# A decoder trunk on one core: layer 0's rows of split activations on another pitch and offset

## The chip, the cores and the metric

One core of a Trainium2 chip. The metric is the device time in microseconds of one execution of the whole program; of the kernel before there are three such runs. One more execution was recorded by the hardware profiler, and all lines of the profile come from that one.

## The reference

Two decoder layers over a sequence of 16 meta tokens and 256 tokens (272 positions), width 2048, 16 heads of 128, an MLP of 8192. All arithmetic is float32. Cut to its core:

```python
for layer in range(2):
    a = rms_norm(h, norm_attn[layer])
    if layer == 0:
        q, k, v, f_logit = split(a @ fox_w_in)          # 2048 x (3*2048 + 16)
        o = forgetting_attention(q, k, v, cumsum(log_sigmoid(f_logit + b_f)))
        h = h + o @ fox_w_o
    else:
        k, v = split(rms_norm(h, kv_norm) @ w_kv)        # 2048 x 4096
        o = stick_breaking_attention(a @ sb_w_q, k, v)
        h = h + o @ sb_w_o
    h = h + square(relu(rms_norm(h, norm_mlp[layer]) @ w_up[layer])) @ w_down[layer]
return rms_norm(h, final_norm)[:, 16:]
```

Layer 0, and the keys and values of layer 1, are computed for all 272 positions; the queries, the output projection and the MLP of layer 1 for the last 256 alone.

## The kernel before

Everything is held feature-major: a tile has 128 features on the partitions and the positions side by side along the partition. A stream of width 2048 is 16 chunks of 128 features.

**Split numbers.** The large products run as three matmuls in fp32r, a form of float32 of which the high part of a number is kept. A weight block is loaded by DMA into `raw` (SP's queue, L202), ScalarE rounds it to `whi` (L213) and VectorE subtracts to get the rest, `wlo` (L214). Activations are split in the same way into `hi` and `lo` (`split_chunk` at L130 and L131, `put_split` at L356 and L357, the MLP's own lines L499 and L500). A product is then whi·hi + whi·lo + wlo·hi, added up in PSUM.

**The rows.** Class `Split` holds both parts of a stream: for each chunk c one row of `XROW` = 576 floats on every partition, with hi from float 16 on and lo directly behind it. With t0 = 0 a part has n = 272 columns, with t0 = M = 16 it has 256:

```python
rows = xs.tile([P, NC, XROW], F32R, tag="x", name=f"x_{label}")
self.hi, self.lo = rows[:, :, XHI:XHI + n], rows[:, :, XHI + n:XHI + 2 * n]
self.both = rows[:, :, XHI:XHI + 2 * n]
```

Pool `xs` has two buffers, which the streams use in turn: x_a (the input of attention), x_o (its output), x_m (the input of the MLP), x_u (four quarters of its inner activations), x_kv (the input of the shared keys and values). The buffer `ob` of the final output comes from the same pool.

**The products.** `gemm_group` (L178) computes 512 output features: 16 chunks of contraction in four blocks `kb`, four output tiles `m`, each with a PSUM tile `acc`. All its matmuls are recorded at L172, in an order that is pinned behind one another. For 272 columns the order is chunk by chunk whi·hi, whi·lo, wlo·hi (L243 to L245). For the 256-column streams (`pairs`) hi and lo lie side by side, so that one matmul of 512 columns (`both`) does whi·hi and whi·lo at once; the 256-column matmuls with wlo follow after the chunks of the run (L231 to L238). The last tile of the last group alone is computed unpaired.

**Order of the work.** The queries, keys and values of layer 0 are computed in groups of four heads, with the small matmuls of attention between them; then output projection, four quarters of the MLP (up, then down), and the same for layer 1. The order on each engine is made by a scheduler when the program is built. All weight tiles have four buffers, so loads and splits run ahead of the matmuls.

**Scratch.** The program reserves 16 KB at the start of each partition for descriptors of DMAs that are written in software; the tiles follow behind it.

Of the kernel before, what the change touches and what calls it, by code (L numbers as in the profile page):

```python
# [9 lines left out]
F32 = mybir.dt.float32  # L10
F32R = mybir.dt.float32r
# [4 lines left out]
P = 128  # L16
D = 2048
NC = D // P
M = 16
# [3 lines left out]
BIG = 1.0e30  # L23
QSCALE = 1.0 / math.sqrt(P)
N_FF = 4
XROW = 576
XHI = 16

G_A0, G_M0, G_KV, G_A1, G_M1, G_FIN = range(6)

# [2 lines left out]
def yoco_kernel(ctx: ExitStack, tc: tile.TileContext, hT_in, gains, b_f, w_f, w_qkv0, w_o0, w_up, w_dn,  # L33
                w_kv, w_q1, w_o1, outT):
    nc = tc.nc
# [6 lines left out]
    xs = ctx.enter_context(tc.tile_pool(name="xs", bufs=2))  # L42
# [74 lines left out]
    class Split:  # L117


        def __init__(self, label, t0):  # L120
            n = T - t0
            self.t0 = t0
            rows = xs.tile([P, NC, XROW], F32R, tag="x", name=f"x_{label}")
            self.hi, self.lo = rows[:, :, XHI:XHI + n], rows[:, :, XHI + n:XHI + 2 * n]
            self.both = rows[:, :, XHI:XHI + 2 * n]

    def split_chunk(sp, gi, c):

# [523 lines left out]
    a, y, t, rs = (fin[:, i, :] for i in range(4))  # L652
# [9 lines left out]
    for i in range(2):  # L662
# [2 lines left out]
            nc.tensor.matmul(pr[:, b * P:(b + 1) * P], rs[:, b:b + 1].to_broadcast([P, P]), ident,  # L665
                             start=True, stop=True)
        prs.append(pr[:, :S])
    ob = xs.tile([P, NC, XROW], F32, tag="x", name="ob")
    pr_sb = tmp.tile([P, T], F32, tag="relu", name="pr_sb")[:, :S]
    nc.scalar.copy(pr_sb, prs[1])  # L670
    for c, n in [(12, 1), (13, 1), (14, 1), (15, 1), (0, 2), (2, 2), (4, 2), (6, 2)]:
# [62 lines left out]
```

## Time and profile before

| | before |
|---|---|
| three runs, us | 2332.77, 2333.07, 2332.89 (median 2332.89) |
| profiled execution, us | 2332.09 |
| its span, first to last instruction, us | 2330.3 |
| granted TensorE clock | 0.998 |
| matmuls | 16,486 |
| busy: TensorE, VectorE, ScalarE, GpSimd | 100%, 58%, 46%, 2% |
| bytes moved by DMA, mean rate | 412.00 MB, 177 GB/s |

Of a matmul the profile gives the start and a duration. The duration runs from the start to the modelled end and overlaps the next matmul, so a stream of matmuls is read by the distance of their starts. In the timeline neighbouring instructions of one kind are merged into one row: start, length of the merged row, engine, line, operation, tiles and number.

Three stretches on the span's scale: layer 0 with its MLP until about 1208 us (its MLP from about 444 us on), the queries, keys, values and attention of layer 1 until about 1532 us, and output projection and MLP of layer 1 until 2318 us.

### The profile page before, as it was taken

Reading aid. Unit: us, or ns where it says so; the run is one execution under the profiler, and the core shown is the slowest. Engines: PE = TensorE matmul, PEld = TensorE weight load, DVE = VectorE, ACT = ScalarE, POOL = GpSimd, SP = SyncE. Lnnn points to the kernel's source line nnn. Section 1 sums busy time; section 2 is a strip of 40 time slices with the busy share of each in tenths; the row PEclk is TensorE's granted clock in tenths of the full one; section 3 lists DMA queues with packets and bytes.
Section 4 is the critical chain, followed back from the end, with each engine's and each line's share of the span. In section 5 each row is a group of like instructions: output and inputs, shape, how many; then the busy total and the mean of one; then the engine's idle time right before and its main releaser. Section 6 shows DMA issues by size and latency. Waiting matters only on the chain.

```text
span 2330.3 us, 39954 instructions
## 1 busy us (share of the span) xinstructions
PE 2319.3 (100%) x16486; PEld 2200.1 (94%) x16486; DVE 1350.6 (58%) x1923; ACT 1064.8 (46%) x1477; POOL 38.9 (2%) x58
## 2 busy tenths in 40 slices
PE   9999999999999999999999999999999999999998
PEld 9999999999999999999998999988888888888887
DVE  7665555654454455445566555566665665655665
ACT  6434344543344344334455444455543543543553
POOL 1000000000000000000000000000000000000000
PEclk9999999999999999999999999999999999999999
DMA  6544545455545555555556444446556556555553
GB/s 233 172 155 163 169 158 171 166 185 173 180 168 185 176 174 180 172 182 172 181 175 198 160 145 145 145 163 199 184 190 198 186 187 199 185 191 195 185 198 128
DMA packets 116630, 412.00 MB, mean 177 GB/s; under 512 B 13264, under 2 KB 16736, under 8 KB 116448
## 3 DMA queue, kind: packets, MB, share of 16 engines
q1 hardware_dynamic: 114560, 406.29, 52.4%
q10 hardware_dynamic: 1888, 3.16, 0.4%
q8 instruction: 129, 2.11, 0.4%
q14 instruction: 53, 0.43, 0.1%
HBM read 407.29 MB, written 2.11 MB: 176 GB/s over the span
## 4 chain that ended last, share of the span: by engine, by line
PE 99%; DVE 0%; ACT 0%; issue 0%; DVEq 0%; ACTq 0%
PE acc L172 96%; PE ps L402 0%; PE pza L581 0%; PE pv L335 0%; PE po L464 0%; PE po L620 0%; PE idle L60 0%; PE pzb L582 0%; PE po L621 0%; PE po L465 0%; PE po L622 0%; DVE ob L676 0%; PE pf L301 0%; PE pf L302 0%; PE pta L597 0%; PE pta L596 0%
## 5 line engine op out<-in xcount | busy, mean ns | idle before, releaser
L214 DVE TENSOR_TENSOR wlo<-raw,whi 128x1024 fp32r<-128x1024 f32 (+1 forms) x773 | 931.7, 1217 | 752.6 <-ACT whi L213 751.7
L213 ACT ACTIVATE whi<-raw 128x1024 fp32r<-128x1024 f32 (+1 forms) x773 | 799.2, 1050 | 960.4 <-PE acc L172 939.9
L172 PE MATMUL acc<-x_u,whi 128*128 128x272 f32 (+2 forms) x3088 | 650.8, 322 | 0.0
L172 PE MATMUL acc<-x_m,whi 128*128 128x272 f32 (+1 forms) x3072 | 649.2, 323 | 0.0
L172 PEld LDWEIGHTS acc<-x_u,whi 128*128 128x128 f32 x3088 | 497.4, 188 | 26.3
L172 PEld LDWEIGHTS acc<-x_m,whi 128*128 128x128 f32 x3072 | 495.5, 188 | 26.9
L172 PE MATMUL acc<-x_u,wlo 128*128 128x272 f32 (+1 forms) x2048 | 441.7, 280 | 0.0
L172 PE MATMUL acc<-x_m,wlo 128*128 128x272 f32 (+1 forms) x2048 | 439.4, 280 | 0.0
L172 PE MATMUL acc<-x_a,whi 128*128 128x272 f32 (+1 forms) x1792 | 363.0, 307 | 0.0
L172 PEld LDWEIGHTS acc<-x_u,wlo 128*128 128x128 f32 x2048 | 339.5, 188 | 15.9
L172 PEld LDWEIGHTS acc<-x_m,wlo 128*128 128x128 f32 x2048 | 338.5, 188 | 16.1
L172 PEld LDWEIGHTS acc<-x_a,whi 128*128 128x128 f32 x1792 | 283.5, 188 | 9.3 <-issue 0.7
L172 PE MATMUL acc<-x_a,wlo 128*128 128x272 f32 (+1 forms) x1024 | 252.9, 284 | 0.0
L172 PE MATMUL acc<-x_kv,whi 128*128 128x272 f32 x1024 | 195.8, 289 | 0.0
L172 PEld LDWEIGHTS acc<-x_a,wlo 128*128 128x128 f32 x1024 | 179.3, 188 | 4.7 <-issue 0.5
L172 PE MATMUL acc<-x_o,whi 128*128 128x272 f32 (+1 forms) x768 | 163.1, 323 | 0.0
L172 PEld LDWEIGHTS acc<-x_kv,whi 128*128 128x128 f32 x1024 | 159.9, 188 | 0.4
L172 PE MATMUL acc<-x_kv,wlo 128*128 128x272 f32 x512 | 145.9, 285 | 0.0
L252 DVE TENSOR_TENSOR hT<-acc,hT 128x256 f32<-128x256 f32 (+1 forms) x239 | 102.5, 429 | 72.0 <-PE acc L172 70.3
L172 PEld LDWEIGHTS acc<-x_o,whi 128*128 128x128 f32 x768 | 124.0, 188 | 6.7
L172 PE MATMUL acc<-x_o,wlo 128*128 128x272 f32 (+1 forms) x512 | 110.8, 282 | 0.0
L172 PEld LDWEIGHTS acc<-x_kv,wlo 128*128 128x128 f32 x512 | 96.2, 188 | 0.1
(226 smaller groups left out, 1038.5 us busy)
## 6 DMA issues: line engine op xcount, KB each, us to landing
raw<-w_up SPq DMA_DIRECT2D x256, 512.0 KB, 4.7
raw<-w_dn SPq DMA_DIRECT2D x256, 512.0 KB, 4.8
raw<-w_qkv SPq DMA_DIRECT2D x92, 512.0 KB, 4.1
raw<-w_o SPq DMA_DIRECT2D x64, 512.0 KB, 4.5
raw<-w_kv SPq DMA_DIRECT2D x64, 512.0 KB, 3.9
raw<-w_q SPq DMA_DIRECT2D x32, 512.0 KB, 4.7
fk<-f_dram ACTq DMA_DIRECT2D x4, 544.0 KB, 5.4
raw<-w_qkv SPq DMA_DIRECT2D x7, 256.0 KB, 4.7
```

The source lines that it names most:

```text
L172: ins = nc.tensor.matmul(*args, **kw).ins
L213: on_act = nc.scalar.activation(hp, src, AF.Copy)
L214: on_dve = nc.vector.tensor_tensor(out=lp, in0=src, in1=hp.bitcast(F32), op=ALU.subtract)
L252: nc.vector.tensor_tensor(out=hT[:, c, t0:], in0=a, in1=hT[:, c, t0:], op=ALU.add)
```

## The change

The rows get a pitch and two offsets of their own for each t0. For the 272-column streams a row has 640 floats (2560 bytes), hi starts at float 48 (byte 192) and lo at float 368 (byte 1472, which is 5 x 256 + 192), so that a gap of 48 floats lies between the parts. For the 256-column streams pitch and offsets stay at 576, 16 and 272 floats. Both kinds share the buffers, which become 16 x 640 + 64 floats long instead of 16 x 576, and `ob` takes the new pitch too. The scratch for software descriptors becomes 1 KB.

```diff
-XROW = 576
-XHI = 16
+ROWS = {0: (640, 48, 368), M: (576, 16, 272)}
+XROW = 640
...
-            rows = xs.tile([P, NC, XROW], F32R, tag="x", name=f"x_{label}")
-            self.hi, self.lo = rows[:, :, XHI:XHI + n], rows[:, :, XHI + n:XHI + 2 * n]
-            self.both = rows[:, :, XHI:XHI + 2 * n]
+            rows = xs.tile([P, NC * XROW + 64], F32R, tag="x", name=f"x_{label}")
+            pitch, hi, lo = ROWS[t0]
+            rows = rows[:, hi:hi + NC * pitch].rearrange("p (c t) -> p c t", c=NC)
+            self.hi, self.lo = rows[:, :, :n], rows[:, :, lo - hi:lo - hi + n]
+            self.both = rows[:, :, :2 * n]
...
-    ob = xs.tile([P, NC, XROW], F32, tag="x", name="ob")
+    ob = xs.tile([P, NC * XROW + 64], F32, tag="x", name="ob")[:, :NC * XROW].rearrange("p (c t) -> p c t", c=NC)
...
-    nc = bacc.Bacc("TRN2", target_bir_lowering=False, num_devices=1)
+    nc = bacc.Bacc("TRN2", target_bir_lowering=False, num_devices=1, dynamic_dma_scratch_size=1024)
```

## The prediction, made before the changed kernel was run

> **What bounds the kernel now.** I read the page first (busy shares, clock, the chain that ended last), then the groups kept apart by shape, the waits, and last the timeline of TensorE in one stretch of each layer.
>
> ```profile
> span 2330.3 us, 39954 instructions
> PE 2319.3 (100%) x16486; PEld 2200.1 (94%) x16486; DVE 1350.6 (58%) x1923; ACT 1064.8 (46%) x1477; POOL 38.9 (2%) x58
> ...
> PEclk9999999999999999999999999999999999999999
> ...
> q1 hardware_dynamic: 114560, 406.29, 52.4%
> q10 hardware_dynamic: 1888, 3.16, 0.4%
> ...
> PE 99%; DVE 0%; ACT 0%; issue 0%; DVEq 0%; ACTq 0%
> ```
>
> TensorE is busy for the whole span at a granted clock of 0.998, and 99% of the chain is TensorE itself: it waits for nobody. The two queues that carry nearly all bytes are hardware queues of SP and ACT. The waits say the same from the other side: the engines that prepare the weights wait for TensorE to give buffers back.
>
> ```profile
> ACT whi L213 <- PE acc L172: 939.9, 482, 4.5
> ```
>
> So time moves only if matmuls follow each other faster or slower. How fast they do is not in the mean duration of a matmul (288 ns, which overlaps its neighbours) but in the spacing of their starts. TensorE in layer 0, where one chunk is whi times hi, whi times lo, wlo times hi (the first two are merged into the "x2" rows):
>
> ```profile
> 700.06 0.28 PE L172 MATMUL acc<-x_m,wlo 128*128 128x272 f32 x1
> 700.18 0.41 PE L172 MATMUL acc<-x_m,whi 128*128 128x272 f32 x2
> 700.44 0.28 PE L172 MATMUL acc<-x_m,wlo 128*128 128x272 f32 x1
> 700.56 0.41 PE L172 MATMUL acc<-x_m,whi 128*128 128x272 f32 x2
> 700.81 0.28 PE L172 MATMUL acc<-x_m,wlo 128*128 128x272 f32 x1
> 700.93 0.41 PE L172 MATMUL acc<-x_m,whi 128*128 128x272 f32 x2
> ```
>
> First column: start in us. From 700.06 to 700.81 are six matmuls, 0.75 us, or 125 ns each; over all 1,024 triples of the x_m rows the raw starts give 373.4 ns a triple, 124.4 ns a matmul. Inside a triple the spacing is not even: a wlo matmul is followed after 0.12 us, the two whi matmuls take 0.25 to 0.26 together. In the raw starts, means: 126.7 ns from whi·hi to whi·lo, 125.8 ns from whi·lo to wlo·hi, 120.9 ns from wlo·hi to the next whi·hi. Column count, weights' size and clock are the same; what differs is where the moving rows stand.
>
> **The addresses.** In the built programs both row buffers begin at a multiple of 256 bytes, before and after. Before, the pitch is 2304 bytes (9 x 256), hi starts 64 and lo 64 + 1088, that is 128, bytes behind a multiple of 256. So the first two spacings lie between rows that stand differently (64 to 128, 128 to 64), the short one between rows that stand alike (64 to 64). After, the pitch is 2560 (10 x 256) and both parts stand at 192: all three spacings are between equals. A row of 272 columns is 1088 bytes; from 192 it ends exactly on a multiple of 256.
>
> **The change part by part.** The programs before and after hold the same instructions in the same order on all five engines; nothing is added, moved or made to wait. Left are four things.
>
> 1. *Layer 0's rows.* They feed the 272-column matmuls of x_a (layer 0's), x_o, x_m, x_u and x_kv: by the groups 1536+768, 512+256, 2048+1024, 2048+1024 and 1024+512, together 10,752, or 3,584 triples. If all three spacings become the equal-standing one, a triple takes 3 x 120.9 = 362.7 ns instead of 373.4: 10.7 ns x 3,584 = 38 us less, all of it on the path. The x_a and x_kv triples keep the same spacing between their attention stretches, so they count in full; the 32 gate matmuls (L301, L302) add 0.1 us at most. Bounds: the best spacing that any row suggests is the timeline's 0.120, which is 4.4 ns less than 124.4, x 10,752 = 48 us less; the worst is every spacing at 126.7 ns, 2.3 ns x 10,752 = 24 us more. I take 120.9, because it is measured on the same shapes.
>
> What is late next if TensorE gains 2%? Nothing: ACT and DVE are busy 46% and 58%, whi preparation idles 940 us waiting for TensorE, and the weight queue takes 52% of the DMA engines.
>
> 2. *ACT and DVE write the rows elsewhere* (L130/L131, L356/L357, L499/L500; 0.42 us each). Their cost at 192 is not in the trace. There are about 250 of them in layer 0's rows (two for each of 16 chunks in x_a, x_m, x_kv and four x_u, 24 in x_o). If each changed by a tenth, 0.04 us, that is 10 us over two engines that idle over 40% of the span: 0, unless they become the last to finish a chunk.
>
> 3. *Scratch of 1 KB instead of 16.* It serves DMAs with descriptors written in software; the page lists only hardware and instruction queues. All tiles move down by 15,360 bytes, and those behind the rows up again by 8,704: multiples of 256, so layer 1's rows, the weights and the attention tiles stand as before. 0.
>
> 4. *The output buffer* has the wider pitch: ten DMAs and ten writes in the last 9 us, rows of 1024 bytes as before. 0, at most 0.1 us either way.
>
> The profiled execution took 2332.09 us, its span 2330.3 and 1.8 around it; the median shown is 2332.89. 2332.09 - 38.3 = 2293.8; against the median 2294.6. I forecast **2294 us**.
>
> **Where this may fail: layer 1.** There all rows stand at 64, equal already:
>
> ```profile
> 1705.33 1.11 PE L172 MATMUL acc<-x_u,wlo 128*128 128x256 f32 x8
> 1706.27 2.00 PE L172 MATMUL acc<-x_u,whi 128*128 128x512 f32 x8
> 1708.10 1.07 PE L172 MATMUL acc<-x_u,wlo 128*128 128x256 f32 x8
> 1709.01 1.99 PE L172 MATMUL acc<-x_u,whi 128*128 128x512 f32 x8
> ```
>
> The same eight wlo matmuls take 0.94 us once (117.5 ns each) and 0.91 the next time (113.8). In the raw starts 46% of the 256-column matmuls run at 113.3 and 50% at 117 to 118.5, and whole runs keep to one of the two. So equal standing does not by itself give the short spacing: there is also a phase into which a run falls.
>
> **Rivals.**
> - *Half-caught phase* (a smaller gain): the good spacing 46% of the time, 0.46 x 48 = 22 us, 2311 us. For it: the two wlo runs above. Against: layer 1 alternates 512 and 256 columns, layer 0 repeats one shape.
> - *No effect.* Where a row starts is indifferent, and the short third spacing only gives back what the first two lost. For it: per triple only the sum is paid, and layer 1's slower wlo spacing, 117.8 for 256 columns, plus 16 columns at 229/512 = 0.45 ns is 125.0, nearly the 124.4 that layer 0's mixed rows pay. 2333 us. [...]
> - *The rear start is dear* (slower). A row that starts at 192 has only 64 bytes before the next multiple of 256, so the first fetch of each matmul brings 16 columns, if fetches go by such blocks. Place: the start of every layer 0 matmul; price: the dearest spacing, 126.7 ns, on all: 24 us more, 2357 us. It decides as soon as the mean spacing passes 124.4 ns. For it: every spacing that touches the row at 128 is 5 ns dearer than the one that does not. Against: the dear spacing before whi·lo and the one behind it are alike, which fits a change of standing better than a bad start.
> [...]
>
> **How the numbers follow.** Full gain 0.43 (2285 to 2300, of it 0.08 for a gain past any row), half-caught 0.18, no effect 0.14, slower 0.25. The likeliest case alone is 2285 to 2311 with its half-caught form. The range: at the bottom the 48 us bound less half a nanosecond of rounding in 0.120 (0.5 x 10.752 = 5 us), 2280; at the top the slower rival's 2357, made 2358. About one in ten lies on either side. 0.2% of the time, 4.7 us, is about what a measurement of this kernel can tell from no change: faster 0.61, same 0.14, slower 0.25.
>
> **What would show it.** In the profile after: TensorE still 100% busy, clock 0.998, instruction counts the same. In layer 0's timeline all three matmuls of a chunk evenly 0.12 apart, a chunk in 0.36 us instead of 0.373; the group of 6,000 matmuls in the chain between 445 and 1209 us shorter by some 22 us; layer 1's eight wlo matmuls still at 0.91 or 0.94. Even spacings at 0.124 would mean no effect; above 0.126 the rear start; a mixture of long and short runs the phase. A new wait of TensorE for wlo, or a changed layer 1, would make my accounting wrong altogether.

## The result, and the profile after

The changed kernel takes 2323.3 us (median of six runs, 2323.03 to 2323.93); the kernel before took 2332.83 beside it. The ratio is 0.996, 95% interval 0.9947 to 0.9973: faster, by 9.5 us where 38 were forecast. The profiled execution took 2323.63 us. Its page, the lines that answer to those shown of before:

```profile
span 2321.9 us, 39954 instructions
PE 2310.8 (100%) x16486; PEld 2190.4 (94%) x16486; DVE 1350.6 (58%) x1923; ACT 1064.0 (46%) x1477; POOL 39.9 (2%) x58
...
PEclk9999999999999999999999999999999999999999
...
q1 hardware_dynamic: 114560, 406.29, 51.4%
q10 hardware_dynamic: 1888, 3.16, 0.4%
...
PE 99%; DMA 0%; DVE 0%; ACT 0%; issue 0%; DVEq 0%; SPq 0%; ACTq 0%
```

Same instructions (39,954), same clock (0.998 of it granted in both), TensorE still the bound. From the waits, ScalarE still waits for TensorE, by some 62 us less:

```profile
ACT whi L217 <- PE acc L176: 877.4, 472, 4.1
```

The timeline of TensorE in the MLP of layer 0 (first column: start; L176 is the old L172):

```profile
700.13 0.28 PE L176 MATMUL acc<-x_m,wlo 128*128 128x272 f32 x1
700.25 0.41 PE L176 MATMUL acc<-x_m,whi 128*128 128x272 f32 x2
700.50 0.29 PE L176 MATMUL acc<-x_m,wlo 128*128 128x272 f32 x1
700.62 0.41 PE L176 MATMUL acc<-x_m,whi 128*128 128x272 f32 x2
700.87 0.28 PE L176 MATMUL acc<-x_m,wlo 128*128 128x272 f32 x1
```

From 700.13 to 700.87 are six matmuls in 0.74 us, where it was 0.75. The spacing is now even, as forecast, but not at the forecast value: the raw starts (the start times as the trace has them, to the nanosecond) give 123.3 to 123.5 ns at each of the three places of a triple, not 120.9. A triple is the three matmuls of one chunk.

The best ruler for a whole stage is a row of the chain in order of time (start, length). One unbroken run has 6,112 matmuls: 6,048 of the 6,144 of layer 0's MLP, which begins at 432.4 us before, and the first 64 of layer 1's queries. Another has 4,020 in the MLP of layer 1. Before:

```profile
444.98 763.71 PE acc L172 x6112
...
1620.80 692.00 PE acc L172 x4020
```

After:

```profile
442.52 757.05 PE acc L176 x6112
...
1610.15 693.91 PE acc L176 x4020
```

Layer 0's run is 6.7 us shorter, and layer 1's, whose rows kept their place, 1.9 us longer. Summed over the distances of all starts: layer 0 and x_kv 1351.9 to 1340.6 us (-11.3), layer 1's other streams 885.2 to 887.4 (+2.2), all other matmuls +0.8. Together this is -8.3, nearly all of the spans' difference of 8.4.

### The profile page after: what moved, and what is told of

Same layout as the page of the kernel before. It is cut to its first block, busy times and chain, and to the rows that moved or that the text cites. A ratio compares the mean times of both kernels' runs of the same rounds, so it can differ in the third digit from the quotient of the medians.

```text
span 2321.9 us, 39954 instructions
## 1 busy us (share of the span) xinstructions
PE 2310.8 (100%) x16486; PEld 2190.4 (94%) x16486; DVE 1350.6 (58%) x1923; ACT 1064.0 (46%) x1477; POOL 39.9 (2%) x58
## 4 chain that ended last, share of the span: by engine, by line
PE 99%; DMA 0%; DVE 0%; ACT 0%; issue 0%; DVEq 0%; SPq 0%; ACTq 0%
PE acc L176 95%; PE ps L406 0%; PE pza L585 0%; PE pv L339 0%; PE po L468 0%; PE po L624 0%; DMA raw<-w_qkv 0%; PE po L625 0%; PE pzb L586 0%; PE po L469 0%; DMA hT<-hT_in 0%; PE po L626 0%; DVE ob L680 0%; PE pf L306 0%; PE pf L305 0%; PE pta L600 0%
## 5 line engine op out<-in xcount | busy, mean ns | idle before, releaser
L176 PE MATMUL acc<-x_u,whi 128*128 128x272 f32 (+2 forms) x3088 | 647.5, 321 | 0.0
L176 PE MATMUL acc<-x_m,whi 128*128 128x272 f32 (+1 forms) x3072 | 646.1, 322 | 0.0
L176 PEld LDWEIGHTS acc<-x_u,whi 128*128 128x128 f32 x3088 | 499.9, 188 | 26.7
L176 PEld LDWEIGHTS acc<-x_m,whi 128*128 128x128 f32 x3072 | 497.8, 188 | 27.4
L176 PE MATMUL acc<-x_u,wlo 128*128 128x272 f32 (+1 forms) x2048 | 445.9, 282 | 0.0
L176 PE MATMUL acc<-x_m,wlo 128*128 128x272 f32 (+1 forms) x2048 | 443.7, 282 | 0.0
L176 PE MATMUL acc<-x_a,whi 128*128 128x272 f32 (+1 forms) x1792 | 360.6, 306 | 0.4 <-ACT x_a L134 0.2
L176 PEld LDWEIGHTS acc<-x_u,wlo 128*128 128x128 f32 x2048 | 340.3, 188 | 15.7
L176 PEld LDWEIGHTS acc<-x_m,wlo 128*128 128x128 f32 x2048 | 339.5, 188 | 15.9
L176 PEld LDWEIGHTS acc<-x_a,whi 128*128 128x128 f32 x1792 | 284.4, 188 | 9.9 <-issue 0.7
L176 PE MATMUL acc<-x_a,wlo 128*128 128x272 f32 (+1 forms) x1024 | 254.5, 286 | 0.0
L176 PE MATMUL acc<-x_kv,whi 128*128 128x272 f32 x1024 | 194.1, 288 | 0.0
L176 PEld LDWEIGHTS acc<-x_a,wlo 128*128 128x128 f32 x1024 | 179.6, 188 | 4.9 <-issue 0.5
L176 PE MATMUL acc<-x_o,whi 128*128 128x272 f32 (+1 forms) x768 | 162.3, 322 | 0.0
L176 PEld LDWEIGHTS acc<-x_kv,whi 128*128 128x128 f32 x1024 | 160.6, 188 | 0.4
L176 PE MATMUL acc<-x_kv,wlo 128*128 128x272 f32 x512 | 147.3, 288 | 0.0
L176 PEld LDWEIGHTS acc<-x_o,whi 128*128 128x128 f32 x768 | 124.3, 188 | 6.8
L176 PE MATMUL acc<-x_o,wlo 128*128 128x272 f32 (+1 forms) x512 | 111.6, 283 | 0.0
L176 PEld LDWEIGHTS acc<-x_kv,wlo 128*128 128x128 f32 x512 | 96.5, 188 | 0.1
```

Of the source, the lines that this page charges most:

```text
L176: ins = nc.tensor.matmul(*args, **kw).ins
```

## The experiments

All are variants of the changed kernel. The place of rows and weights is given in bytes behind a multiple of 256; in the changed kernel the weights whi and wlo stand at 0. The distance between rows and weights is the difference of their places, again modulo 256. Rows are "equal" when hi and lo have the same place, and "mixed" when they have not. "Run of layer 0" and "run of layer 1" are the two chain rows, each from the one profiled execution of its kernel. The expectations count in units of 0.417 ns, which they call cycles; no run shows a step of that length. 304, 298.7 and 296 of them are 126.7, 124.4 and 123.3 ns, and go with runs of layer 0 of 777, 764 and 757 us.

### Is it equal standing, or 192?

```diff
-ROWS = {0: (640, 48, 368), M: (576, 16, 272)}
+ROWS = {0: (640, 16, 336), M: (576, 16, 272)}    # both_at_64
+ROWS = {0: (640, 0, 320), M: (576, 16, 272)}     # both_at_0
+ROWS = {0: (640, 32, 352), M: (576, 16, 272)}    # both_at_128
+ROWS = {0: (640, 16, 288), M: (576, 16, 272)}    # wide_pitch_64_128
```

> Layer 0's hi and lo both 64 bytes behind a multiple of 256, pitch 640 floats as in the changed kernel. Theory A (equal standing is what pays, whichever the offset): spacing of layer 0's matmuls 123.3 to 123.4 ns as with 192, time 2323. Theory B (192 pays, because a row of 1088 bytes then ends on a multiple of 256 and touches one partial block): 64 has two partial blocks (192 and 128 bytes) and stays at 124.4 ns, 2333. Theory C (starts fall into a repeating pattern of their own for each offset): some other mean, 120 to 125 ns, 2290 to 2340, with layer 1 moving by a few us as well.

> Both parts at a multiple of 256. Theory A: 2323, 123.4 ns. Theory B: four whole blocks and one partial block of 64 bytes at the end, as good as 192: 2323. If the short first fetch of 192 is what helps (and not the number of blocks): worse than 192, 124.4 ns or more, 2333 or more. Theory C: some other mean, 120 to 125 ns.

> Both parts at 128. Theory A: 2323, 123.4 ns. Theory B: two partial blocks (128 at the start, 192 at the end): 124.4 ns, 2333. Theory C: some other mean, 120 to 125 ns.

> The offsets of before (hi 64, lo 128) on the new pitch of 2560 bytes, with the new scratch and buffer size: all of the change but the offsets. All theories: layer 0 at 124.4 ns. If layer 1's loss (256-column spacing 115.8 before, 116.5 after, 1.7 us) comes from its shifted buffers, it shows here too: 2334 to 2335. If it comes from the phase in which layer 0 leaves TensorE, layer 1 is as before: 2333. If the pitch itself matters, the time differs from 2333 by over 3 us.

Measured: at 64 2355.1 us (ratio 1.0095, 1.008 to 1.011), at 0 2351.7 (1.0079, 1.0064 to 1.0094), at 128 2355.5 (1.0096, 1.0079 to 1.0112), the old offsets on the new pitch 2333.2 (1.0001, 0.9991 to 1.001). The timeline of the kernel with both parts at 64:

```profile
700.19 0.29 PE L176 MATMUL acc<-x_m,wlo 128*128 128x272 f32 x1
700.32 0.42 PE L176 MATMUL acc<-x_m,whi 128*128 128x272 f32 x2
700.57 0.29 PE L176 MATMUL acc<-x_m,wlo 128*128 128x272 f32 x1
700.70 0.42 PE L176 MATMUL acc<-x_m,whi 128*128 128x272 f32 x2
700.95 0.29 PE L176 MATMUL acc<-x_m,wlo 128*128 128x272 f32 x1
```

and its run of layer 0:

```profile
450.83 777.16 PE acc L176 x6112
```

Here too the spacing is even, and six matmuls take 0.76 us: each of the three takes 126.7 ns. That is the dearest spacing of before, now at the place where before had its cheapest (64 to 64). So theory A falls, and with it the reading of the 120.9 ns: that spacing was no price of a pair of rows but a place in a pattern of which only the sum is paid. Theory B falls as well: by its own count 0 touches as few blocks as 192, and it is slow (2351.7 us against 2323.3). All three slow kernels come to the same value in layer 0's MLP (runs of layer 0 with rows at 64, 0 and 128: 777.16, 777.21, 777.16 us). Where 0 is quicker than 64 and 128, by 3.4 us and more, it is outside that run, in the x_a, x_o and x_kv rows; layer 0 and x_kv add up to 1368.9 us at 0, and to 1373.7 and 1374.4 at 64 and 128. The fourth kernel frees scratch, pitch and buffer sizes from any part in it; its run of layer 1 is 692.00 us, so layer 1's loss does not come from the moved buffers either.

### The rows' own place, or their distance to the weights?

```diff
-    pad = align.tile([P, 32], F32, name="pad")
+    pad = align.tile([P, 48], F32, name="pad")       # weights_at_64 and all_shifted_64
...
-ROWS = {0: (640, 48, 368), M: (576, 16, 272)}
+ROWS = {0: (640, 32, 352), M: (576, 0, 256)}         # weights_at_64 alone
```

> The alignment tile before the weight tiles is 64 bytes longer, so whi and wlo stand at 64 instead of 0 behind a multiple of 256; the offsets inside the rows are cut by 64 bytes, so layer 0's rows stay at 192 and layer 1's at 64. Theory D (only the moving rows' own place counts): 123.4 ns in layer 0, 2323 to 2325. Theory E (what counts is the rows' place relative to the weights that are loaded meanwhile, now 128): the spacing of the 128 rows, 126.7 ns, 2355; layer 1 (relative place 0 instead of 64) moves too.

> The alignment tile is 64 bytes longer and nothing else: weights at 64, layer 0's rows at 0, layer 1's rows at 128 behind a multiple of 256; the distances between rows and weights (192 and 64) are those of the changed kernel. Theory D (the rows' own place): layer 0 at 126.7 ns as with rows at 0, 2352. Theory E (the distance between rows and weights): 123.4 ns, 2323, and layer 1 as in the changed kernel.

Measured: with the weights alone moved 2367.8 us (1.0148, 1.0133 to 1.0163); with weights and rows moved together 2322.1 (0.9953, 0.9938 to 0.9968). The chain's runs, first of the kernel with the weights alone moved:

```profile
451.35 777.27 PE acc L176 x6112
...
1645.78 701.52 PE acc L176 x4020
```

and of the one in which all moved together:

```profile
441.79 757.03 PE acc L176 x6112
...
1609.48 692.00 PE acc L176 x4020
```

The first kernel reads its rows from exactly the places of the changed kernel (192 and 64) and loses 20 us in layer 0's run and 7.6 in layer 1's. The second has rows at 0 (layer 0) and 128 (layer 1). With the weights at 0 a place of 0 was bad in layer 0, and the last experiment will show 128 to be bad in layer 1; here nothing is lost. Theory E holds: what decides is the distance between moving rows and weights. The longer alignment tile also moves the tiles behind the rows by 64 bytes. They are not the cause: the last experiment moves wlo by 64 bytes and no other tile off its place, and layer 0 pays the same.

Moving the weights alone by 64 bytes, with the rows left in their places, cost 44 us against the changed kernel (2367.8 against 2323.3).

### How wide is the good place?

```diff
-ROWS = {0: (640, 48, 368), M: (576, 16, 272)}
+ROWS = {0: (640, 56, 376), M: (576, 16, 272)}    # both_at_224
+ROWS = {0: (640, 40, 360), M: (576, 16, 272)}    # both_at_160
+ROWS = {0: (640, 44, 364), M: (576, 16, 272)}    # both_at_176
```

> Layer 0's parts at 224: 32 bytes before a multiple of 256, which is not a multiple of 64. If reads go in 64-byte pieces, each row of 1088 bytes now touches 18 pieces instead of 17: a piece lasts 6.67 ns (16 columns; the spacings seen are 304 = 19 x 16, 296 = 18.5 x 16 and 298.7 cycles of 0.417 ns), so up to 6.7 ns a matmul more than with 192, 130 ns, 2395. If pieces are 32 bytes or less and only the 256-byte block counts: like 192, 2323 or a little less.

> Layer 0's parts at 160, again not a multiple of 64. With 64-byte pieces: 18 pieces a row, up to 6.7 ns a matmul more than with 128 (126.7) or 192 (123.4): 130 to 133 ns, 2395 to 2430. With smaller pieces: between the 126.7 ns of 128 and the 123.4 ns of 192, 2323 to 2355.

> Layer 0's parts at 176, between 160 and 192, which both gave 296 cycles a matmul. If that is a plateau from 160 to 192: 296 cycles, 123.4 ns, 2323. If the fetch goes by finer steps, with an optimum between: 288 to 292 cycles, 120 to 122 ns, 2287 to 2305.

Measured: 224 takes 2353.2 us (1.0085, 1.007 to 1.01), 160 takes 2323.6 (0.9957, 0.9941 to 0.9974), 176 takes 2322.2 (0.9952, 0.9935 to 0.9969). Runs of layer 0: 777.17, 757.05 and 757.05 us. These rows are, for 224, 160 and 176 in this order:

```profile
448.33 777.17 PE acc L176 x6112
...
442.48 757.05 PE acc L176 x6112
...
443.76 757.05 PE acc L176 x6112
```

In this run there are two values and nothing between them: good at 160, 176 and 192, bad at 224, 0, 64 and 128. Reads in 64-byte pieces, reckoned as for 160, would have made 160 worse than 128, and a finer optimum would have shown at 176; neither did. The run of layer 1 is 692.00 us with 176 and 693.91 with 192, though no row of layer 1 moved; each value is from one execution, so that no gain of 176 over 192 is shown.

### Do the weight loads take part at all?

```diff
-    gemm_matmul(accs[m][:, :n], wh, lo, start=False, stop=False)
-    gemm_matmul(accs[m][:, :n], wl, hi, start=False, stop=kb == kc == 3)
+    gemm_matmul(accs[m][:64, :n], wh[:, :64], lo, start=False, stop=False)
+    gemm_matmul(accs[m][:64, :n], wl[:, :64], hi, start=False, stop=False)
...
```

> Changed kernel, but in the unpaired matmuls (layer 0 and x_kv) whi times lo and wlo times hi load and use only the first 64 of 128 weight columns: half of the small corrections is left out, so the output is less exact. In the last chunk of a group whi times hi comes last. Rows, number of moving columns and number of matmuls are as in the changed kernel. Theory D (the reads of the moving rows alone set the spacing): 123.4 ns as before, 2323. [...]

One run was made, 2336.9 us, with this run of layer 0:

```profile
447.43 764.15 PE acc L176 x6112
```

That is 7 us more than with full loads, 124.5 ns a matmul where it was 123.3. Theory D does not have this. The shorter loads do take less time (135 instead of 188 ns in the x_u rows), and the rows were read alike, so D is out. Had the loads simply held the moving rows back, as I also thought possible, shorter ones would have made layer 0 faster; its run became longer, 764.15 us where it was 757.05. That speaks against a plain sharing of bandwidth. The edit halves the output rows that these matmuls write as well, and their part in it was not tried alone.

### Mixed rows: does each matmul pay for itself?

```diff
-ROWS = {0: (640, 48, 368), M: (576, 16, 272)}
+ROWS = {0: (640, 48, 320), M: (576, 16, 272)}    # hi192_lo0
+ROWS = {0: (640, 48, 336), M: (576, 16, 272)}    # hi192_lo64
+ROWS = {0: (640, 48, 352), M: (576, 16, 272)}    # hi192_lo128
+ROWS = {0: (640, 16, 304), M: (576, 16, 272)}    # hi64_lo192
```

> Changed kernel with layer 0's lo at 0 and hi at 192. Theory H (each matmul pays by the distance of its own rows to the weights: 296 cycles at 160 to 192, 304 at 0, 64, 128, 224): two of three at 296, one at 304, mean 298.7 cycles, 124.4 ns, 2334. Theory I (only the pattern of the whole sequence counts, which repeats with the triple): another mean, 288 to 304 cycles, not the one that H adds up; the kernel before already speaks for I, with 298.7 for 64 and 128 where H gives 304.

> lo at 64, hi at 192. Theory H: 298.7 cycles, 124.4 ns, 2334. Theory I: another mean than that, 288 to 304 cycles, 2287 to 2355.

> lo at 128, hi at 192. Theory H: 298.7 cycles, 2334. Theory I: another mean, 288 to 304 cycles, 2287 to 2355.

> hi at 64, lo at 192, so only one matmul in three (whi times lo) reads rows at the good distance. Theory H: two of three at 304, one at 296: 301.3 cycles, 125.6 ns, 2346. Theory I: another mean, 288 to 304 cycles.

Measured: 2334.8, 2335.0, 2335.3 and 2335.1 us (ratios 1.0006 to 1.001, each interval within 0.9997 to 1.002). Their runs of layer 0 are 763.76, 763.75, 763.77 and 763.73 us: 124.4 ns, and nearly the 763.71 us of the kernel before with 64 and 128. The first and the last of the four:

```profile
444.79 763.76 PE acc L176 x6112
...
445.02 763.73 PE acc L176 x6112
```

Theory H gets the first three right and misses the last (124.4 where it says 125.6) and the kernel before (it says 126.7). Theory I, which wanted other means, misses too. What stands is simpler: in layer 0's MLP mixed rows cost 373.3 ns a triple in the mean, in all five mixtures that were run; equal rows cost 370.0 or 380.0, by their distance to the weights. Single spacings, and even single triples, go up and down without any effect on this mean. In the kernel with lo at 64, for instance, raw starts are 124, 120 and 133 ns apart in one triple and 123, 125 and 123 in the next, 377 and 371 ns in all.

### Layer 1, and wlo apart from whi

```diff
-ROWS = {0: (640, 48, 368), M: (576, 16, 272)}
+ROWS = {0: (640, 48, 368), M: (576, 48, 304)}    # layer1_at_192
+ROWS = {0: (640, 48, 368), M: (576, 32, 288)}    # layer1_at_128
...
-    wlo = wspl.tile([P, 2, 512], F32R, tag="wlo", name=f"wlo_{u}_{kb}_{hf}")
+    wlo = wspl.tile([P, 1088], F32R, tag="wlo", name=f"wlo_{u}_{kb}_{hf}")
+    o1 = 32 if pairs else 0      # wlo128_layer1, with layer 0's rows at 176; wlo64_everywhere: 16
+    wlo = wlo[:, o1:o1 + 1024].rearrange("p (k c) -> p k c", k=2)
```

> Changed kernel with layer 1's 256-column rows (hi and lo side by side, 512 together) at 192 too. Its own layer 1 at 64: 512 columns 230.2 ns, 256 columns 116.5 ns, 887.4 us in all; at distance 0 (the run with weights at 64) 231.5 and 118.9, 897 us. Theory E with one good distance for all lengths: layer 1 shorter, towards 113.3 ns and 226 ns in every run: up to 18 us, 2305. If the good distance depends on the length: layer 1 like 64 or worse, 2323 to 2345.

> Changed kernel with layer 1's rows at 128. One good distance for all lengths (about 160 to 192) would make 128 bad here as in layer 0: layer 1 at 2 to 4 ns more a matmul, 2333 to 2345. If it depends on the length, anything from 2305 to 2345.

> Changed kernel with layer 0's rows at 176 (as good as 192 so far) and, in layer 1's paired groups alone, the wlo tiles shifted to 128 behind a multiple of 256, whi left at 0. Layer 1's rows stay at 64: distance 64 to whi (where 512 columns took 230.0 ns), 192 to wlo (where 256 columns took 114.4 ns with rows at 192). If the distance to the weights loaded meanwhile decides, piece by piece: layer 1 at 230.0 and 114.4 ns, 881.6 us, 3.6 us less than the best so far, 2318. If the sequence as a whole decides, layer 1 lands on another mean, 880 to 897 us, 2317 to 2333. If wlo's place is indifferent: 885.2 or 887.4 us, 2322 or 2323.

> Changed kernel with wlo at 64 and whi at 0; rows at 192 (layer 0) and 64 (layer 1). In layer 0 the distances to the weights are then mixed, 192 to whi and 128 to wlo, although both parts of the rows stand alike. If mixed distances give what mixed rows gave in five kernels: 298.7 cycles, 124.4 ns in layer 0; layer 1 has distance 0 to wlo and pays 118 to 119 ns for 256 columns: 2335 to 2345. If wlo's place is indifferent: 296 cycles, 2323.

The columns "512 columns" and "256 columns" are mean distances from one start to the next.

| kernel | us | ratio, interval | 512 columns, ns | 256 columns, ns | run of layer 1, us |
|---|---|---|---|---|---|
| changed kernel, rows at 64 | 2323.3 | 0.996, 0.9947 to 0.9973 | 230.2 | 116.5 | 693.91 |
| layer1_at_192 | 2324.2 | 0.9961, 0.9946 to 0.9976 | 232.7 | 114.4 | 694.66 |
| layer1_at_128 | 2334.6 | 1.0008, 0.9998 to 1.0017 | 231.9 | 119.1 | 702.74 |
| wlo128_layer1 | 2330.1 | 0.999, 0.9981 to 0.9998 | 232.3 | 116.7 | 698.67 |
| wlo64_everywhere | 2360.9 | 1.0121, 1.0105 to 1.0136 | 229.9 | 117.9 | 696.53 |

Which distance is good depends on the sequence: 192 helps the 256-column matmuls and hurts the 512-column ones, 64 remains best for layer 1, and 128 is bad for both. Giving each its own (wlo128_layer1) did not add the two up: the 512-column matmuls, whose rows and own weights had not moved, became 2 ns slower. So layer 1 too answers as a whole sequence. With wlo at 64 everywhere layer 0 gets the bad value:

```profile
450.81 777.21 PE acc L176 x6112
```

Its rows are at the good distance from whi and at a bad one (128) from wlo: wlo's distance counts. I had expected the 124.4 ns of mixed rows there; equal rows at mixed distances to the weights do not behave like mixed rows. Whether whi's distance counts by itself in layer 0 stays open.

## Why the prediction was right and wrong, step by step

**What bounds the kernel, and what is late next.** Right. TensorE is 100% busy before and after and makes up 99% of the chain in both, and the kernels differ by the spacing of their matmuls. The one exception is the start: in the changed kernel the chain's first 12 us run through the loads of the input and of the first weights. That is worth little: the run of layer 0 starts at 441.50 to 442.52 us in the three kernels in which layer 0 is laid out as in the changed kernel, to the byte.

**Part 1, the term that failed.** The forecast took 120.9 ns, the one spacing between rows that stood alike, as what all three would cost. The mechanism under it, equal standing, is refuted: equal rows at 64 cost 126.7 ns at every place of the triple. The prediction said that only the place of the moving rows differed between the three spacings; but the weights that are loaded differ too, two of whi to one of wlo. The kernel with wlo at 64 shows that uneven spacings need no unequal rows: its hi and lo both stand at 192, and its means are 122.7, 125.8 and 131.7 ns. What the change did earn, 11.3 us for 10,752 matmuls or 1.05 ns each where 3.5 were forecast, comes from something that the prediction had not named: 192 is a good distance from the weights for this sequence, and 64 mixed with 128 lies between good and bad. With both parts at 64, the natural way to make them equal, the same reasoning would have forecast the same 38 us of gain and met a loss of 22. That the kernel got faster at all is luck: it comes from the choice of 192, not from the argument.

**Parts 2 to 4.** Right: pitch, scratch, output buffer and the place of the writes are worth nothing that can be measured (2333.2 us with all of them and the old offsets).

**Layer 1 "as before".** Its addresses were, its time was not: 2.2 us more. The two patterns that the prediction showed there, 113 and 118 ns, are the reason: the share of 256-column matmuls that are followed after 113 or 114 ns fell from 47% to 32%. Layer 1's run is 692.00 us in six of the kernels that left the distance between its rows and the weights alone, the kernel before among them, and 693.91 in nine, and nothing between. all_shifted_64, in which all distances are those of the changed kernel, has 692.00, and so has both_at_176. That the phase at the end of layer 0 picks the pattern is a reading that was argued, not shown. Nor is it shown that the value belongs to the kernel: each was profiled once, and other executions of the same kernel may fall into the other pattern.

**The rivals.** "The rear start is dear" is refuted, since 192 is among the good places and 0 a bad one. "No effect" is refuted as well: with the weights at 0 and both parts at 160, 176 or 192 the run of layer 0 takes 757 us, at 0, 64, 128 and 224 it takes 777: where a row starts is not indifferent. In the numbers "no effect" (2333 us) came nearest, 10 us off, and "half-caught phase" (2311) was 12 off; the forecast was 29 off. A gain past any row, to which the prediction gave 0.08, did not show: no layout got layer 0's MLP below 123.3 ns a matmul. "Half-caught phase" is wrong in kind too: layer 0's MLP runs in one even pattern, 123.3 to 123.5 ns at each place of the triple, not in two. The sentence under "no effect" that only the sum of a triple is paid was the truest of the text, and should have stopped me from using one third of a triple as a price. The layer 1 rows, equal at 64 and yet at the high value half of the time, were the second warning.

## What to carry to other kernels

When matmuls follow each other without a wait, read the mean spacing of a whole repeating sequence; a short spacing inside it is not a price that the others could have (120.9 ns here, where no layout got the mean below 123.3). If a stream of fp32r matmuls keeps TensorE busy throughout, try the offset of the moving rows against the weight tiles, modulo 256 bytes, a few values for each shape: here the layouts range from 0.5% faster to 1.5% slower than the kernel before, with the same instructions, and a pad that moved the weights alone by 64 bytes cost 44 us against the changed kernel. Try the whole sequence, since what was best for each shape alone did not add up.

## What the runs showed of the hardware

- In layer 0's MLP the mean spacing of the 272-column matmuls took three values in all kernels but half_weights: 370.0, 373.3 and 380.0 ns a triple, which is 55.5, 56 and 57 times 6.67 ns. What a step of 6.67 ns would be, no run shows.
- Where weights and moving rows stand to each other, modulo 256 bytes, changes the rate of the matmuls: 757.0 or 777.2 us for the same 6,112 when the rows are equal. Multiples of 256 made no difference where they were tried: the wider pitch with the old offsets moves the rows of the chunks by different ones, and the run of layer 0 stays at 763.71 us. The cause below the distance is open: shorter weight loads made the run slower (764.15 us), and no run shows why the distance counts.
- The fastest layouts found are the changed kernel's with 176 in place of 192 (2322.2 us) and with everything moved by 64 bytes (2322.1 us). They were not timed beside the changed kernel's 2323.3, and their intervals overlap with its own: that they are faster than it is not shown. Their one profiled execution each has the shorter run of layer 1 (692.00 against 693.91 us).
